# The first x and y tiles of an interleaving kernel, loaded in column halves in turn

## The chip, the cores and the metric

The kernel runs on one core of a Trainium2 chip. The metric is the device time of one execution in microseconds (us); lower is better. Times are medians of several runs; a profile is taken in one execution of its own.

## What is computed

Two float32 arrays x and y of shape (32, 256, 1024) are interleaved along the last axis, so that the result has 2048 columns:

```python
result = np.zeros((batch, seq, dim * 2), dtype=np.float32)
result[..., 0::2] = x
result[..., 1::2] = y
```

There is no arithmetic. Each input has 33.55 MB and the output 67.11 MB, so that 67.11 MB are read and 67.11 MB written.

## The kernel before

Each input is looked at as a flat run of numbers and cut into `n` = 8 tiles of 128 partitions by `W` = 8192 floats (32 KB in each partition, 4 MB in all). One tile of x and one of y give 8 MB of output, which is made in two halves: the half `h` (0 or 1) takes `H` = 4096 columns of x and of y and gives an output tile of 128 x 8192, 4 MB.

There are two buffers for x (`xt`), two for y (`yt`), used by even and odd tiles, and two for the output (`ot`), one for each half. Three engines run lists of their own, held together by semaphores:

- SP issues all loads. The x tile 0 comes in two column halves (L37 and L38, counted by `xsem[0]` and `hsem`), every other tile whole (x at L45, y at L48). From tile 2 on, a load of x waits until the third weave of the tile two before it is done, and a load of y until the fourth is, so that the buffer is free (L43 and L47).
- DVE weaves. For each tile and half, one copy spreads x to the even columns of `ot[h]` (L60) and one spreads y to the odd columns (L63). Ahead of the x copy it waits for the load of x and, from tile 1 on, for the store that last used `ot[h]` (L59); ahead of the first y copy of a tile it waits for the load of y (L62). Each copy counts `woven` up by one.
- ACT issues all stores (L68), one for each half, after the second copy of that half.

Each load and each store is spread over the core's 16 DMA engines, 8 of the 128 partition rows to each. In the profile q1 is the queue of SP's loads, and q10 that of ACT's stores.

After the program is built, the first two loads of SP are moved ahead of the barrier with which the program opens (L89 to L107); the loads after them are issued behind it.

Of the kernel before, what the change touches and what calls it, by code (L numbers as in the profile page):

```python
# [3 lines left out]


def _interleave(nc, x, y, out):
    P = 128
    W = 8192
    H = W // 2  # L10

    total = 1
    for s in x.shape:
        total *= s
    n = total // (P * W)
    assert n * P * W == total

    def rows(ap, names, k):
        flat = ap.rearrange("b s d -> (b s d)")
        return flat[k * names : (k + 1) * names].rearrange("(p w) -> p w", p=P)  # L20

    fp32 = mybir.dt.float32
    xt = [nc.alloc_sbuf_tensor(f"xt{b}", [P, W], fp32).ap() for b in (0, 1)]
    yt = [nc.alloc_sbuf_tensor(f"yt{b}", [P, W], fp32).ap() for b in (0, 1)]
    ot = [nc.alloc_sbuf_tensor(f"ot{b}", [P, W], fp32).ap() for b in (0, 1)]

    xsem = [nc.alloc_semaphore(f"xsem{b}") for b in (0, 1)]
    hsem = nc.alloc_semaphore("hsem")
    ysem = [nc.alloc_semaphore(f"ysem{b}") for b in (0, 1)]
    woven = nc.alloc_semaphore("woven")  # L30
    osem = [nc.alloc_semaphore(f"osem{b}") for b in (0, 1)]

    xs = [rows(x, P * W, k) for k in range(n)]
    ys = [rows(y, P * W, k) for k in range(n)]
    os_ = [rows(out, 2 * P * W, k) for k in range(n)]

    nc.sync.dma_start(out=xt[0][:, :H], in_=xs[0][:, :H]).then_inc(xsem[0], 16)  # L37
    nc.sync.dma_start(out=xt[0][:, H:], in_=xs[0][:, H:]).then_inc(hsem, 16)  # L38

    for k in range(n):  # L40
        b = k % 2
        if k >= 2:
            nc.sync.wait_ge(woven, 4 * (k - 2) + 3)  # L43
        if k:
            nc.sync.dma_start(out=xt[b], in_=xs[k]).then_inc(xsem[b], 16)  # L45
        if k >= 2:
            nc.sync.wait_ge(woven, 4 * (k - 2) + 4)  # L47
        nc.sync.dma_start(out=yt[b], in_=ys[k]).then_inc(ysem[b], 16)  # L48

    for k in range(n):  # L50
        b = k % 2
        for h in (0, 1):
            c = slice(h * H, (h + 1) * H)
            if h == 0:
                nc.vector.wait_ge(xsem[b], 16 * (k // 2 + 1))
            elif k == 0:
                nc.vector.wait_ge(hsem, 16)
            if k:
                nc.vector.wait_ge(osem[h], 16 * k)  # L59
            nc.vector.tensor_copy(out=ot[h][:, 0::2], in_=xt[b][:, c]).then_inc(woven, 1)  # L60
            if h == 0:
                nc.vector.wait_ge(ysem[b], 16 * (k // 2 + 1))  # L62
            nc.vector.tensor_copy(out=ot[h][:, 1::2], in_=yt[b][:, c]).then_inc(woven, 1)  # L63

    for k in range(n):
        for h in (0, 1):
            nc.scalar.wait_ge(woven, 4 * k + 2 * h + 2)
            nc.scalar.dma_start(  # L68
                out=os_[k][:, h * W : (h + 1) * W], in_=ot[h]
            ).then_inc(osem[h], 16)  # L70

    nc.scalar.wait_ge(osem[0], 16 * n)
    used = sorted(s.num for s in [*xsem, hsem, *ysem, woven, osem[0]])
    assert used == list(range(used[0], used[-1] + 1)), used
    nc.scalar.sem_clear(range(used[0], used[-1] + 1))
    nc.sync.nop(nofuse=True).wait_op(osem[1], 16 * n, "sem-ge").then_inc(
        osem[1], -16 * n
    )


def kernel(tc, x, y, out):
    nc = tc.nc
    tc.close()
    tc.compile()

    _interleave(nc, x, y, out)

    blocks = nc.main_func.blocks
    for engine in (mybir.EngineType.SP, mybir.EngineType.SP):  # L89
        opening = blocks[0].instructions  # L90
        at, moved = next(
            (b, i)
            for b in blocks[1:]
            for i in b.instructions
            if i.engine == engine and i.opcode == "DMACopy"
        )
        assert not (moved.sync_info and moved.sync_info.on_wait)
        body = at.instructions
        body.remove(moved)
        gate = next(  # L100
            n
            for n, i in enumerate(opening)
            if i.engine == engine and i.opcode == "Drain"
        )
        opening.insert(gate, moved)
        at.instructions = body
        blocks[0].instructions = opening  # L107


# [1 line left out]
_INS = ['x', 'y']  # L111
_OUTS = [((32, 256, 2048), 'float32')]


# [23 lines left out]
```

## Time and profile before

| | before |
|---|---|
| time, median of 3 runs | 314.31 us (314.28 to 314.42) |
| the profiled execution | 314.29 us |
| its span, first to last instruction | 313.0 us |
| DVE busy | 72.6 us (23%), 32 copies |
| one copy L60, L63 | 2295 ns, 2292 ns |
| DMA | 134.22 MB, mean 429 GB/s |
| loads (q1), stores (q10), share of the 16 DMA engines' span | 50.1%, 49.7% |
| DVE's idle time before L60, before L63 | 178.8 us, 46.7 us |

The span is what the profile covers; the time of an execution is a little longer. Nothing runs on TensorE. Idle time of DVE is put down to the transfer that ended it. In the windows view, each line gives a stretch of the span, its length, the busy time of the engines with their number of instructions, the clock, the mean busy share of the DMA engines and the rate in GB/s. The records of single packets, which lie under these views in the trace, give each packet's start, duration, size and queue.

The opening, by the timeline: the loads are issued at 0.00 and 0.42 (the x halves), 1.90 (y), 2.28 and 2.76 us (tile 1). DVE weaves the first x half from 7.30 and the first y half from 21.90, and the first store is issued at 24.23.

### The profile page before, as it was taken

The numbers are of one execution on the slowest core, as the hardware profiler recorded it, in microseconds if no ns is written. First come the engines' busy times: TensorE is split into PE (matmuls) and PEld (weight loads), VectorE is DVE, ScalarE is ACT, GpSimd is POOL, SyncE is SP. The second block draws the span as 40 slices with busy tenths as digits, with TensorE's granted clock in tenths as the row PEclk, the third lists the DMA queues.
The fourth block names the chain that finished last, engine by engine and source line by source line (L and its number), as shares of the span: only waits on it lengthen the run. The fifth ranks groups of instructions, "written<-read, shape, count | busy, mean of one in ns | idle before, by whom it ended". The sixth has DMA issues, their size and how long they took to land.

```text
span 313.0 us, 113 instructions
## 1 busy us (share of the span) xinstructions
DVE 72.6 (23%) x32; POOL 0.2 (0%) x4
## 2 busy tenths in 40 slices
DVE  0226002231022410325003150031501305013510
POOL 0000000000000000000000000000000000000000
DMA  8999999999999999999999999999999999999998
GB/s 341 463 410 394 469 402 448 423 436 436 419 452 406 465 402 469 402 469 402 469 402 448 423 436 436 419 452 406 465 402 469 402 469 402 465 406 444 427 431 373
DMA packets 4752, 134.22 MB, mean 429 GB/s; under 512 B 528, under 2 KB 528, under 8 KB 528
## 3 DMA queue, kind: packets, MB, share of 16 engines
q1 hardware_dynamic: 2448, 67.11, 50.1%
q10 hardware_dynamic: 2304, 67.11, 49.7%
HBM read 67.11 MB, written 67.11 MB: 429 GB/s over the span
## 4 chain that ended last, share of the span: by engine, by line
DMA 82%; DVE 12%; issue 0%
DMA out_dram<-ot 76%; DVE ot L63 6%; DMA yt<-in_y_dram 6%; DVE ot L60 6%
## 5 line engine op out<-in xcount | busy, mean ns | idle before, releaser
L60 DVE COPY ot<-xt 128x4096 f32<-128x4096 f32 x16 | 36.7, 2295 | 178.8 <-DMA out_dram<-ot 171.5
L63 DVE COPY ot<-yt 128x4096 f32<-128x4096 f32 x16 | 36.7, 2292 | 46.7 <-DMA yt<-in_y_dram 46.7
L122 POOL MEMSET const-bfloat16-1.0<- 128x1 bf16 x1 | 0.1, 101 | 0.0
L122 POOL MEMSET const-uint8-127<- 128x1 uint8 x1 | 0.1, 101 | 0.0
L122 POOL MEMSET const-float32-0.0<- 128x1 f32 x1 | 0.1, 98 | 0.2 <-issue 0.2
L122 POOL MEMSET const-float32-1.0<- 128x1 f32 x1 | 0.1, 98 | 0.0
## 6 DMA issues: line engine op xcount, KB each, us to landing
out_dram<-ot ACTq DMA_DIRECT2D x16, 4096.0 KB, 29.1
yt<-in_y_dram SPq DMA_DIRECT2D x8, 4096.0 KB, 60.8
xt<-in_x_dram SPq DMA_DIRECT2D x7, 4096.0 KB, 43.7
xt<-in_x_dram SPq DMA_DIRECT2D x2, 2048.0 KB, 9.5
```

What stands on the lines that cost most here:

```text
L60: nc.vector.tensor_copy(out=ot[h][:, 0::2], in_=xt[b][:, c]).then_inc(woven, 1)
L63: nc.vector.tensor_copy(out=ot[h][:, 1::2], in_=yt[b][:, c]).then_inc(woven, 1)
L122: nc = _bacc.Bacc("TRN2", target_bir_lowering=False, num_devices=1)
```

## The change

The first y tile is loaded in two column halves too, and the four halves come in the order x, y, x, y. The second y half has a semaphore of its own, `qsem`, and DVE waits for it ahead of the second y copy of tile 0. The whole load of y tile 0 in the loop falls away. The two loads that are moved ahead of the opening barrier are still the first two of SP, now the first x half and the first y half.

```diff
+    qsem = nc.alloc_semaphore("qsem")
...
     nc.sync.dma_start(out=xt[0][:, :H], in_=xs[0][:, :H]).then_inc(xsem[0], 16)
+    nc.sync.dma_start(out=yt[0][:, :H], in_=ys[0][:, :H]).then_inc(ysem[0], 16)
     nc.sync.dma_start(out=xt[0][:, H:], in_=xs[0][:, H:]).then_inc(hsem, 16)
+    nc.sync.dma_start(out=yt[0][:, H:], in_=ys[0][:, H:]).then_inc(qsem, 16)
...
-        nc.sync.dma_start(out=yt[b], in_=ys[k]).then_inc(ysem[b], 16)
+        if k:
+            nc.sync.dma_start(out=yt[b], in_=ys[k]).then_inc(ysem[b], 16)
...
             if h == 0:
                 nc.vector.wait_ge(ysem[b], 16 * (k // 2 + 1))
+            elif k == 0:
+                nc.vector.wait_ge(qsem, 16)
             nc.vector.tensor_copy(out=ot[h][:, 1::2], in_=yt[b][:, c]).then_inc(woven, 1)
...
-    used = sorted(s.num for s in [*xsem, hsem, *ysem, woven, osem[0]])
+    used = sorted(s.num for s in [*xsem, hsem, qsem, *ysem, woven, osem[0]])
```

## The prediction

> **What bounds the kernel now.** I read the page first: its rows of DMA and of DVE, the queues, then the groups of instructions.
>
> ```profile
> DVE 72.6 (23%) x32; POOL 0.2 (0%) x4
> DMA  8999999999999999999999999999999999999998
> DMA packets 4752, 134.22 MB, mean 429 GB/s; under 512 B 528, under 2 KB 528, under 8 KB 528
> q1 hardware_dynamic: 2448, 67.11, 50.1%
> q10 hardware_dynamic: 2304, 67.11, 49.7%
> L60 DVE COPY ot<-xt 128x4096 f32<-128x4096 f32 x16 | 36.7, 2295 | 178.8 <-DMA out_dram<-ot 171.5
> L63 DVE COPY ot<-yt 128x4096 f32<-128x4096 f32 x16 | 36.7, 2292 | 46.7 <-DMA yt<-in_y_dram 46.7
> ```
>
> DVE, the only engine that computes, is busy for 23% of the span and waits for transfers the rest of it. The DMA engines are busy in every slice, and the loads (q1) and stores (q10) fill 99.8% of them between them. So the question is not when a store may start but when the 16 engines are empty. The windows view, in stretches of 12.1 us, tells whether the mix of loads and stores matters (columns: stretch, length, DVE and POOL busy, clock, DMA share, GB/s):
>
> ```profile
> 12.00:24.10 12.10, 2.20 (x1) 0.00 (x0) 1.00 1.00 433
> 24.10:36.20 12.10, 4.50 (x3) 0.00 (x0) 1.00 0.96 390
> 48.30:60.40 12.10, 4.30 (x2) 0.00 (x0) 1.00 1.00 433
> 299.90:312.00 12.10, 0.00 (x0) 0.00 (x0) 1.00 1.00 433
> ```
>
> Loads alone (12 to 24), both together (48 to 60), stores alone (300 to 312): 433 GB/s each time. Only the stretch in which the first store joins the loads is slower. In steps of 1.21 us, the time of one 32 KB packet on an engine, it looks like this:
>
> ```profile
> 25.12:26.33 1.21, 1.21 (x2) 0.00 (x0) 1.00 1.11 433
> 26.33:27.54 1.21, 1.21 (x2) 0.00 (x0) 1.00 1.22 352
> 27.54:28.75 1.21, 1.06 (x1) 0.00 (x0) 1.00 0.27 81
> 28.75:29.96 1.21, 0.00 (x0) 0.00 (x0) 1.00 1.02 433
> ```
>
> There is one hole in the stream, just ahead of the first store packet (29.06 us; its store was issued at 24.23). The steps count packets by their start, so the view bounds the hole by one step, 1.21 us. The records of the single packets are finer: the last two load packets on each engine before the hole took on average 1.35 and 1.80 us instead of 1.213, and the first store packet 1.23. That is 0.14 + 0.58 + 0.02 = 0.74 us lost.
>
> **The account of the run before.** On each engine: first packet at 1.01 us; 256 steps of 1.2094 us (packet start to packet start) = 309.6; 33 small closing packets of 0.006 = 0.2; the first packets' slow start 0.58 (1.19 us on average for 16 KB that later take 0.611); the hole 0.74. Sum 312.1; the last packet ends at 312.58, the rest being the engines' spread (their first packets start over 0.5 us). Landing and closing make it 313.0, and 1.29 lies outside the span: 314.29, against a median of 314.31.
>
> **The change, part by part.** *Bytes and packets.* The same 134.22 MB. The first y tile comes in 16 KB packets, 16 per engine instead of 8 of 32 KB. The x halves of before show 16 KB packets 0.607 us apart: 16 x 0.607 - 8 x 1.2094 = +0.04, and one more closing packet 0.006. Together **+0.05 us**.
>
> *Issues.* L37 stays first at 0.00; the y half takes L38's place (0.42), the second x half that of the first y load (1.90), and the second y half comes one issue later, near 2.3, which pushes the loads of tile 1 back by 0.4 us. The two early halves keep the engines busy until 11.3 to 11.8 us, so everything issued by 3.7 us is covered by 7.6 us of queued work: 0. If that cover were gone, each issue would cost its 0.33 to 0.44 us.
>
> *The first store.* The y half lands where the second x half did (L38's landing, 12.16). Weave 2.3 us: store issued at 14.5 instead of 24.23, 9.7 us sooner. Its first packet comes 4.83 us after issue if it goes as before, or 3.6 if the two load packets ahead of it count 0.61 each instead of 1.21: at 18.1 to 19.3. No byte goes faster for that: from there the loads run at half pace, as in the mixed stretch. By the 433 GB/s of every mix this is 0. The new wait of DVE for the second y half holds nothing up but the second store.
>
> *What is late next: stores run out.* Before, both stores of tile 0 were issued by 28.65, and each later store while others were queued. After the change I walk it by packets, alternating between the queues as the records show in the mixed stretch. x, second half: packets end at 16.6, woven by 19.3. y, second half: 2 to 5 of its 8 packets are through when the store enters; each other one shares with a 32 KB store packet (0.61 + 1.21 = 1.82 us), ends 24.8 to 28.1, lands 1.59 later (y1: packets end 53.61, landed 55.20), woven 2.3 later: second store issued at 28.7 to 32.0. The first store's last packet starts 32.3 to 35.7. In the early corner the second store's issue comes only 0.3 us before that, and a store needed over 1 us from issue to engine: the store queue may run empty for 2 us here. Then, surely: the second store ends at 53 to 57, while the next needs the whole of y1. By then the engines have moved 32 steps of loads and 16 of stores: 1.6 + 48 x 1.21 + 0.74 = 60.4; landed 60.8, woven 63.1. So q10 is empty from about 55 until 66 to 68. The loads of tile 2 were long released (their weaves ended at 19.3 and about 31), so the engines go on at 433 GB/s, loads alone. But the store queue must be entered anew, once for sure and perhaps twice.
>
> *The price of an entry.* Only one is in the trace, 0.74 us. Another costs between 0 (the delay belonged to the very first use of the queue) and 1.21 us (the view's bound). I take 0.74: the hole lies where an empty queue's first packet has to come, and the other empty queue that is filled, that of loads at the start, shows a slow first packet of nearly the same size (0.58 lost), while transfers queued behind others show none. The first entry, now among 16 KB packets, I leave at 0.74; two shorter packets ahead could hide up to 1.21 less of it (worse), or it could vanish (better).
>
> *The end.* After its late entry the first store of tile 1 stands to the loads as the first store of tile 0 did before: woven from the last full y tile, 4.83 us after issue. So the rest repeats the old rhythm. Its last piece: store 15 of 16 was issued at 289.9, and store 14's last packet ended at 293.22, 3.3 us later, of which a fresh issue needs 1.0 (L37 to its first packet). The 2.3 us left cover it. Losing all of it and 2.3 more would cost 2.3; I count 0.
>
> **Sum:** 314.3 + 0.05 + 0.74 = **315.1 us** with one new entry, 315.8 with two.
>
> **Rivals.**
> *The entry costs only once per run* (the store queue's first use), so the refill is free: 314.3 + 0.05 = 314.35, no change. For it: one hole in the whole trace. Against: no other empty store queue is in the trace to compare. It decides from an entry price below 0.58 us (0.63 less 0.05).
> *Faster:* with smaller packets in flight the first entry finds a gap at once and loses nothing, and the later one is warm: 314.3 + 0.05 - 0.74 = 313.6. It needs both. Nothing shows the first.
> *The early store is worth its lead:* 9.7 us off, 304.6. The account excludes it: 309.6 us of packets do not fit.
> *Each added transfer pays a fixed cost* of an undrained queue, 1.01 from issue to packet and 0.36 from packet to landing: 315.7. The x halves speak against it: the second's packets follow the first's with one closing packet of 0.006 us between. The Trainium skill (DMA: Bandwidth & Descriptors, "Anatomy of one DMA — SWDGE (gpsimd) path") gives every transfer about 2.0 us fixed beside its bytes; taken for these loads too, as an estimate, the added split would make it 316.3. This trace shows that cost hidden for transfers that queue.
> *The change does not do what it says:* the early place goes to the first two loads of SP, now an x and a y half; DVE and ACT keep their order. Only a late y half would undo it.
>
> **How the numbers follow.** About 0.2% (0.63 us) can be told from no change here. New entries cost: 0.55, of which 0.05 at a price too small to tell. Free refill: 0.36. Faster: 0.04. Fixed cost, 0.03; a wider first hole alone, 0.02. The lead that pays and the undone change, under 0.01, are inside these. So faster 0.04, same 0.36 + 0.05 = 0.41, slower 0.50 + 0.03 + 0.02 = 0.55. The forecast is one new entry, 315.1. The range runs from the free refill less a little, 314.2, to two entries and some more at the first, 316.0; the slower case's own range is 314.9 to 316.0.
>
> **What would show it.** In the profile after: the first store issued near 14.5; 433 GB/s in all stretches but those around 17 and around 66 us (perhaps 35); a stretch near 60 with loads alone; the tail as before, with DVE's wait before its last weave near 3.8 us. No dip near 66 and 314.4 would be the first rival. Wrong altogether: a stretch under 433 GB/s in the steady part or after the last load, or a bandwidth above it anywhere.

## The result and the profile after

The changed kernel takes 314.86 us (median of 22 runs, 314.66 to 315.09), the kernel before 314.44 us beside it (22 runs). The ratio is 1.0014, 95% interval 1.0008 to 1.0020: slower by 0.42 us. The interval excludes 1, and yet this is less than the 0.2% (0.63 us) that the prediction set as the least that could be told from no change. The profiled execution took 314.66 us against 314.29.

The page of the changed kernel, the lines that answer to those of before (L65 and L70 are the weaves of x and y):

```profile
DMA  8999999999999999999999999999999999999998
DMA packets 4896, 134.22 MB, mean 428 GB/s; under 512 B 544, under 2 KB 544, under 8 KB 544
q1 hardware_dynamic: 2592, 67.11, 50.2%
q10 hardware_dynamic: 2304, 67.11, 49.6%
L65 DVE COPY ot<-xt 128x4096 f32<-128x4096 f32 x16 | 36.7, 2295 | 171.8 <-DMA out_dram<-ot 146.0
L70 DVE COPY ot<-yt 128x4096 f32<-128x4096 f32 x16 | 36.7, 2292 | 53.9 <-DMA yt<-in_y_dram 53.9
```

Little in it has moved but the packets: 144 more, 128 of them data and 16 closing ones. DVE waits as long as ever, 225.7 us against 225.5, with 7 us moved from the x weaves to the y weaves. The timeline of the opening shows that the change does what it says:

```profile
12.28 2.30 DVE L70 COPY ot<-yt 128x4096 f32<-128x4096 f32 x1 [2.56 <-DMA yt<-in_y_dram]
14.60 82.39 ACTq L75 DMA_DIRECT2D out_dram<-ot  x5
17.17 2.30 DVE L65 COPY ot<-xt 128x4096 f32<-128x4096 f32 x1 [2.60 <-DMA xt<-in_x_dram]
30.17 2.30 DVE L70 COPY ot<-yt 128x4096 f32<-128x4096 f32 x1 [10.70 <-DMA yt<-in_y_dram]
```

The first store is issued at 14.60 instead of 24.23. In the windows view, around the first store (steps of one packet time) and around the later refill of the store queue:

```profile
14.52:15.73 1.21, 0.05 (x1) 0.00 (x0) 1.00 1.01 433
15.73:16.94 1.21, 0.00 (x0) 0.00 (x0) 1.00 0.97 393
16.94:18.15 1.21, 0.98 (x1) 0.00 (x0) 1.00 1.28 311
18.15:19.36 1.21, 1.21 (x1) 0.00 (x0) 1.00 1.14 393
19.36:20.57 1.21, 0.11 (x1) 0.00 (x0) 1.00 0.66 284
...
65.21:66.42 1.21, 1.21 (x2) 0.00 (x0) 1.00 1.00 433
66.42:67.63 1.21, 1.21 (x1) 0.00 (x0) 1.00 1.00 433
67.63:68.84 1.21, 0.69 (x1) 0.00 (x0) 1.00 1.00 433
68.84:70.05 1.21, 0.00 (x0) 0.00 (x0) 1.00 1.00 433
```

The hole at the first store is there again: the four steps below 433 GB/s lack as much as the full stream moves in 0.98 us. At 68.14 us the first store packet of tile 1 enters a queue that had been empty since 53.99 us, and the stream does not falter.

For finer numbers I use the records of the single packets. *Loss* below is the time that has gone by, less the work of the packets done by then at their undisturbed spacing (1.2094 us for 32 KB, 0.607 for 16 KB, 0.006 for a closing packet, other sizes in proportion), as the mean of the 16 engines. What it grows by around a hole is what the hole costs. By it the last packet's end moves from 312.58 to 312.97 us, by 0.39:

| term | before | after | difference |
|---|---|---|---|
| the y split, 16 KB spacing and a closing packet | | | +0.05 |
| opening (loss at 8 us) | 1.84 | 1.91 | +0.07 |
| first store (growth) | 0.76 | 1.00 | +0.24 |
| refill at 68 us (growth) | none there | 0.00 | 0.00 |
| after the last load, to the last packet | 0.14 | 0.17 | +0.03 |

In four kernels below whose opening is that of the kernel before, the loss at 8 us is 1.87 to 1.96, each from one profile; the 0.07 is no larger than that scatter, and no run shows it to be an effect of the change. So the first store's hole is the large term, and the next question is what makes it 1.00 instead of 0.76.

### The profile page after: what moved, and what is told of

Same layout as the page of the kernel before. It is cut to its first block, busy times and chain, and to the rows that moved or that the text cites. A ratio compares the mean times of both kernels' runs of the same rounds, so it can differ in the third digit from the quotient of the medians.

```text
span 313.3 us, 114 instructions
## 1 busy us (share of the span) xinstructions
DVE 72.7 (23%) x32; POOL 0.2 (0%) x4
## 4 chain that ended last, share of the span: by engine, by line
DMA 79%; DVE 12%; another core or an unknown queue 4%; SPq 0%; issue 0%
DMA out_dram<-ot 65%; DMA xt<-in_x_dram 15%; DVE ot L65 6%; DVE ot L70 6%; SPq L42 0%; SPq L41 0%
## 5 line engine op out<-in xcount | busy, mean ns | idle before, releaser
L65 DVE COPY ot<-xt 128x4096 f32<-128x4096 f32 x16 | 36.7, 2295 | 171.8 <-DMA out_dram<-ot 146.0
L70 DVE COPY ot<-yt 128x4096 f32<-128x4096 f32 x16 | 36.7, 2292 | 53.9 <-DMA yt<-in_y_dram 53.9
```

## The experiments

Theories are numbered as they came up. The diffs show the lines that matter; `...` stands for lines left out, among them those that allocate a semaphore or count it. The kernel before, run beside them, had medians of 314.46 to 314.52 us.

### The store queue used earlier by a load

```diff
-    nc.sync.dma_start(out=xt[0][:, H:], in_=xs[0][:, H:]).then_inc(hsem, 16)
+    nc.scalar.dma_start(out=xt[0][:, H:], in_=xs[0][:, H:]).then_inc(hsem, 16)
```

> The kernel before, with the load of the second x half issued by ACT instead of SP, so that the store queue (q10) carries a load at about 2 us and is empty again well before the first store. Theory 1 (the hole is the price of the queue's very first use): no hole near 26 us; 0.75 us lost among the load packets near 3 us instead (time 314.4, as before) or nothing at all there (313.6). Theory 2 (the hole is the price of the first packet that goes from SBUF to DRAM, whatever its queue did before): hole of 0.75 us still at 26 us, time 314.4.

314.45 us, ratio 1.0003 (0.9994 to 1.0011). q10 carried the x half from 5.62 to 17.73 us (the second early place went to the load of y tile 0, at 0.41). The hole stands where it was, with a growth of 0.81:

```profile
26.40:27.61 1.21, 1.21 (x2) 0.00 (x0) 1.00 1.16 325
27.61:28.82 1.21, 1.03 (x1) 0.00 (x0) 1.00 0.36 108
```

Theory 1, the queue's first use, is out.

### A tiny store ahead of the first

```diff
+    warm = nc.alloc_sbuf_tensor("warm", [16, 128], fp32).ap()
+    nc.vector.memset(warm, 0.0).then_inc(wset, 1)
...
+    nc.scalar.wait_ge(wset, 1)
+    nc.scalar.dma_start(out=os_[0][:16, :128], in_=warm).then_inc(wsem, 16)
+    nc.scalar.wait_ge(wsem, 16)
...
```

> The kernel before, with a store of 16 rows of 512 bytes issued by ACT at about 2 us into a place that the first real store overwrites later. Theories 1 and 2 both say that the hole near 26 us is gone; what it cost is paid at the start. If the opening, in which the engines wait for their first data anyway, hides it: 313.7 to 313.9. If it is paid among the x packets at its full price: 314.4. Theory 3 (each filling of an empty store queue costs 0.74, as the prediction took it) says that the hole stays at 26 us and the tiny store adds one: 315.0.

314.44 us, ratio 1.0002 (0.9993 to 1.0011). Its 512-byte packets went out from 5.66 us without a visible loss, and the hole near 26 us stayed, 0.60. Theory 2, the first packet from SBUF to DRAM, is out. Theory 3 is hit too: the tiny store filled an empty queue and added no hole.

The same with 128 rows, so that each engine has used the partitions and output rows of the real store, from a buffer of its own and from `ot` itself (there DVE zeroes the 512 bytes first, and weaves only when the tiny store has landed):

> The kernel before, with a store of 128 rows of 512 bytes issued by ACT at about 2 us, from a tile of its own into the place that the first real store overwrites; so every engine has read its own partitions and written its own output rows before. Theory 4 (the hole is a first touch by each engine of its partitions or of its output rows): the hole near 26 us, 0.6 to 0.8 us in four kernels so far, is gone, 313.8. Theory 5 (a first touch of the output buffer ot as a source): the hole stays, 314.5. Theory 6 (the first store packet is late because of its own 32 KB, wherever it goes): the hole stays.

> As the run before it, but with the tiny store read from the first 512 bytes of each row of ot, the buffer of the first real store. Theories 4 and 5: the hole near 26 us is gone, 313.8 to 313.9. Theory 6: it stays, 314.5.

314.56 us (ratio 0.9996 to 1.0015) and 314.48 us (0.9994 to 1.0012); holes of 0.64 and 0.84. Theories 4 and 5, a first touch of rows or buffer, are out as far as 512 bytes of each row can touch them.

### The store queue emptied four times

```diff
             nc.scalar.wait_ge(woven, 4 * k + 2 * h + 2)
+            if h == 0 and 2 <= k <= 5:
+                nc.scalar.wait_ge(osem[1], 16 * k)
```

> The kernel before, with ACT waiting ahead of the first store of tiles 2, 3, 4 and 5 until the store before it has landed, so that the store queue runs empty four times beside queued loads. Theory 3 (each filling costs 0.74): +3.0 us, 317.4, with a hole in the stream at each. Theories 1 and 2 (only the first costs): within 0.2 us of before, 433 GB/s at each of the four refills, with loads alone for a few us ahead of each.

318.2 us, ratio 1.0122 (1.0108 to 1.0136). That is near Theory 3's time (317.4), and yet not for its reason. The first refill (110 us) and the third (196 us) grew the loss by 0.00, the second (153 us) by some 0.04. The packets show where it went: the load queue ran dry from 236.12 to 242.74 us, because its next loads were issued only at 237.56 and 239.76, behind weaves of which the first had waited 15.0 us for a store; the loss grew by 2.5 us from 230 to 260, and by 1.1 at the end, where the last packets of the 16 engines end between 315.2 and 316.6 us. Another 0.5 went between 128 and 220 us, apart from the refills; what took it is not known. The windows of the first refill, of this stretch and of the end:

```profile
104.00:116.10 12.10, 4.50 (x2) 0.00 (x0) 1.00 1.00 433
238.10:250.20 12.10, 1.63 (x1) 0.00 (x0) 1.00 1.00 387
304.00:316.10 12.10, 0.00 (x0) 0.00 (x0) 1.00 0.92 398
```

The median alone would have been read as a confirmation. The edit disturbed more than it was meant to; only its first three refills come beside loads that run on.

### The packets in flight

The load of x tile 1, which is in flight when the first store of the kernel before comes, in two halves:

```diff
-        if k:
+        if k == 1:
+            for c in range(2):
+                s = slice(c * 4096, (c + 1) * 4096)
+                nc.sync.dma_start(out=xt[b][:, s], in_=xs[k][:, s]).then_inc(psem, 16)
+        elif k:
...
```

> The kernel before, with the load of x tile 1 in two column halves, so that the load packets in flight when the first store comes have 16 KB, not 32. If the packets' size sets how much of the first store's delay is covered: the hole grows from 0.75 to 1.0 us, and with the split's 0.05 the time is +0.3, 314.7. If the size has no part in it and the hole of the changed kernel was longer because it came early: hole 0.75, time +0.05, 314.45.

The hole grew to 0.98, at 26 us, with the store issued at 24.31:

```profile
25.71:26.92 1.21, 1.21 (x2) 0.00 (x0) 1.00 1.23 420
26.92:28.13 1.21, 1.21 (x1) 0.00 (x0) 1.00 1.08 244
28.13:29.34 1.21, 0.55 (x1) 0.00 (x0) 1.00 0.93 379
29.34:30.55 1.21, 0.00 (x0) 0.00 (x0) 1.00 0.66 284
```

The early time is not needed for the wider hole; the smaller packets are enough. The time rose more than forecast, to 315.05 us, ratio 1.0019 (1.0010 to 1.0028), and the rest of it, 0.39, lies at the end:

```profile
291.21:292.42 1.21, 1.21 (x1) 0.00 (x0) 1.00 1.00 433
292.42:293.63 1.21, 0.45 (x1) 0.00 (x0) 1.00 0.19 81
293.63:294.84 1.21, 0.64 (x1) 0.00 (x0) 1.00 1.01 433
```

Beside 32 KB store packets, 16 KB load packets get a third of an engine instead of half (from 29 to 34 us, 43 load packets start and 41 store packets), so the loads end at 288.98 us instead of 285.96. Store 15 is issued at 292.90, store 14's last packet ends at 293.82, and 0.92 us is too little: the engines stand idle. This is the cushion at the end that the prediction put at 2.3 us, here used up.

The opposite, on the changed kernel: the whole load of x tile 1 ahead of the second halves, so that 32 KB packets are in flight when the early store comes:

```diff
     nc.sync.dma_start(out=yt[0][:, :H], in_=ys[0][:, :H]).then_inc(ysem[0], 16)
+    nc.sync.dma_start(out=xt[1], in_=xs[1]).then_inc(xsem[1], 16)
     nc.sync.dma_start(out=xt[0][:, H:], in_=xs[0][:, H:]).then_inc(hsem, 16)
...
-        if k:
+        if k >= 2:
             nc.sync.dma_start(out=xt[b], in_=xs[k]).then_inc(xsem[b], 16)
```

> The changed kernel, with the whole load of x tile 1 put between the first and the second halves, so that 32 KB load packets are in flight when the early first store comes. If the packets' size sets the first hole (as the run with x tile 1 in halves showed near 26 us): the hole falls from 1.00 to 0.75 us, and with it the time by 0.25, to 314.6. If the early time sets it: 1.00 stays, 314.86.

The hole fell to 0.76, as forecast, though the store came as early as in the changed kernel (first packet 19.45 us):

```profile
16.92:18.13 1.21, 0.00 (x0) 0.00 (x0) 1.00 1.47 433
18.13:19.34 1.21, 0.00 (x0) 0.00 (x0) 1.00 0.00 0
19.34:20.55 1.21, 0.00 (x0) 0.00 (x0) 1.00 1.00 433
...
43.00:55.10 12.10, 3.55 (x2) 0.00 (x0) 1.00 1.00 433
```

The last line is a refill: the store queue was empty from 34.41 to 48.54 us, and again nothing is lost. The times fall into two groups, 314.43 to 314.55 (six runs) and 315.10 to 315.94 (six); the profile, 314.47, is of the lower, and what makes the upper is not known. The median of 314.82 decides nothing.

The split without the turn-taking:

```diff
-    nc.sync.dma_start(out=yt[0][:, :H], in_=ys[0][:, :H]).then_inc(ysem[0], 16)
     nc.sync.dma_start(out=xt[0][:, H:], in_=xs[0][:, H:]).then_inc(hsem, 16)
+    nc.sync.dma_start(out=yt[0][:, :H], in_=ys[0][:, :H]).then_inc(ysem[0], 16)
```

> The changed kernel with its first four loads in the order x, x, y, y: the split alone, without the turn-taking; the first store then starts some 5 us later than in the changed kernel and 5 us sooner than before. If the cost comes from the 16 KB packets in flight and the split: first hole 1.0 us near 21 us, time as the changed kernel, 314.8 to 314.9. If it comes from the turn-taking or the early time: hole 0.75, 314.5.

It was a poor test. The store was issued at 19.55 us, and by its first packet (24.35) the loads in flight were those of x tile 1, 32 KB each; the hole was 0.75, as their size would have it, and by my wording this would have spoken for the turn-taking. The time missed both forecasts: 316.08 us, ratio 1.0045 (1.0031 to 1.0058), spread from 314.84 to 316.98. The profile, 315.08, has a refill at 67.16 us that did cost something, 0.48, and loses 0.31 us after the last load, where the kernel before loses 0.14. Why the split alone is slower than the changed kernel in most runs stays open.

### The store's own packets

The first store in two pieces, 8 KB and 24 KB of each row:

```diff
+            if k == 0 and h == 0:
+                for s in (slice(0, 2048), slice(2048, 8192)):
+                    nc.scalar.dma_start(
+                        out=os_[0][:, s], in_=ot[0][:, s]
+                    ).then_inc(fsem, 16)
+                continue
...
```

> The kernel before, with the first store in two pieces, 8 KB and then 24 KB of each row, so that the first store packet has 8 KB instead of 32. Theory 6 (the packet must be read before the engine can go on): the hole shrinks from 0.75 to about 0.2 us or less, 313.9. Theories 4 and 5: it stays at 0.6 to 0.8, 314.5.

The hole shrank to 0.40, and 0.17 more came at the step to the second piece: 314.22 us, ratio 0.9991 (0.9982 to 1.0000). Theory 6 holds in sign, not in size. With 2 KB and 30 KB (`slice(0, 512)`):

> The kernel before, with the first store in two pieces of 2 KB and 30 KB of each row. The piece of 8 KB left 0.40 us of hole and 0.16 us at the step to 24 KB. If the first packet's own size sets the hole: 0.3 us or less at the first piece, about 0.2 at the step to 30 KB; time 314.1 to 314.2. If the hole goes with the first packet of near 32 KB, wherever it stands: next to none at the first piece, 0.6 or more at the step; time 314.4.

0.02 at the first piece and 0.79 at the step to the second (its first packet at 39.47 us). The windows view of that stretch:

```profile
34.00:46.10 12.10, 0.00 (x0) 0.00 (x0) 1.00 0.96 387
```

314.38 us, ratio 0.9995 (0.9986 to 1.0003). The hole waits for the large packets, in a queue that by then is not empty. The same cut as the first, on the changed kernel (8 KB and 24 KB):

> The changed kernel, with its first store in two pieces of 8 KB and 24 KB of each row. If the store packet's own size is a part of the hole here too: 1.00 falls by about 0.35 to 0.65 us, and 0.1 to 0.2 comes at the second piece; time 314.6 to 314.7. If in this kernel the hole is set by the load packets alone: 1.00, 314.9.

1.00 fell to 0.47, and 0.24 more came at the step to the second piece (first packet at 27.72 us): 314.55 us, ratio 1.0003 (0.9994 to 1.0011), with 0.31 lost again at the end. So the size of the first store's packets counts in both kernels.

Is one large packet enough?

```diff
+        if k == 2:
+            nc.sync.wait_ge(wsem, 16)
...
+    nc.scalar.wait_ge(xsem[0], 16)
+    nc.scalar.dma_start(out=os_[0][:16, :H], in_=xt[0][:16, :H]).then_inc(wsem, 16)
+    nc.scalar.wait_ge(wsem, 16)
```

> The kernel before, with an early store of one 16 KB packet per engine (16 rows, raw x) as soon as the first x half is there, about 7.3 us; it writes a place that the first real store overwrites later. Theory 7 (only the first large store packet on an engine makes a hole): a hole near 10 us, and less than 0.2 us, or none, near 26; the time 0.6 us (one packet more) above before, 315.0. Theory 8 (the hole belongs to the first lasting stream of stores, not to a first packet): 0.6 to 0.8 us near 26 us as ever.

The one packet per engine at 10.9 us lost 0.03, and the hole near 26 us stayed, 0.61. That is as Theory 8 has it, the first lasting stream of stores. The time, 315.2 us (ratio 1.0011 to 1.0031), is 0.7 us above the kernel before, of which the added packet explains 0.6.

### The holes together

| load packets in flight | growth of loss at the first whole store, us |
|---|---|
| 32 KB, nine kernels | 0.60 to 0.84 |
| 16 KB: the changed kernel, x tile 1 in halves | 1.00, 0.98 |

The first row has before (0.76), the x half on ACT, the three tiny stores, the four gaps (0.65), x tile 1 first (0.76), the split alone (0.75) and the early large packet (0.61). The rows do not overlap, and the size was changed both ways, each time with the store's time left alone. Each figure is of one profile.

The same profiles show how the hole is made up. Beside 32 KB load packets the first store packet came 4.68 to 4.92 us after its issue, and less the hole that leaves 4.04 to 4.16 us in all nine: by this reckoning the loads ran on for that long. Beside 16 KB packets it came after 4.51 and 4.56 us, and the loads ran on for only 3.51 and 3.58: smaller packets cover half a microsecond less.

## Why the prediction was right or wrong

**What bounds the kernel: right.** 9.7 us of an earlier store bought nothing. Every stretch of loads alone, of both and of stores alone ran at 433 GB/s in the changed kernel too. Its 452 GB/s from 24.00 to 36.10 us is no rate above the bound: the view counts packets by their start, and the loss stays at 2.9 us over that stretch.

**The walk: mostly right.** First store issued at 14.60 (14.5 predicted), its first packet at 19.11 (18.1 to 19.3), the next tile's first store packet at 68.14 (66 to 68), and DVE's wait ahead of the last weaves as before, 3.76 us. The second y half came later than said: packets end at 28.58 (24.8 to 28.1), second store issued at 32.49. The queue did not visibly run empty for it: its first packet came 2.27 us after the first store's last packet ended, 2.10 in the undisturbed alternation.

**The price of an entry: wrong, and with it the forecast's main term.** The prediction put 0.74 us on the refill at 68 us and left the first entry as it was. The refill cost 0.00. The first entry cost 0.24 more, because 16 KB packets were in flight; the prediction had named this ("two shorter packets ahead could hide up to 1.21 less of it") and counted it as nothing, with 0.02 for it alone. So 0.05 + 0.24, and 0.07 of scatter in the opening, took the place of 0.05 + 0.74: the forecast of 315.1 us lay near the measured 314.86 by luck, with a wrong term inside. The first rival was right on the refill, though its reason, the queue's first use, was ruled out by the x half on ACT; its 314.35 missed the wider hole.

**Its reasoning on the price.** That "the hole lies where an empty queue's first packet has to come" was an argument from one event. Refills of the empty store queue beside loads cost 0.00 (the changed kernel at 68 us, x tile 1 first at 48, the gaps at 110 and 196), 0.04 (the gaps at 153) and 0.48 (the split alone at 67). An empty queue is not enough to make a hole. In the five refills beside loads that cost 0.04 at most, the first packet came 3.05 to 4.19 us after its issue, within the 4.04 to 4.16 that the loads covered at the first store, or nearly so; in the one that cost 0.48 it came after 4.47. Why the first store's packet takes longer is not shown.

**The other rivals.** A fixed cost of 1.4 us for each added transfer is out: the whole difference is 0.39 us, of which the packets of the split account for 0.05. The Trainium skill (DMA: Bandwidth & Descriptors, "Anatomy of one DMA — SWDGE (gpsimd) path") gives about 2.0 us fixed for each DMA on the GpSimd path. These loads are issued by SP and queue behind others, and no such cost shows in their time. The faster rival's smaller packets did the reverse of what it needed.

**Shown and open.** Shown: the hole of the first lasting stream of large stores grows when the load packets in flight get smaller and shrinks when its own first packets do. Not shown: why. Theory 6, that a store packet must first be read before the engine can go on, fits the sign of both, but no record here tells a packet's reading from its writing, and it does not tell why later entries of the same size were mostly free. This stays open, as do the two groups of times of x tile 1 first and the spread of the split alone.

## What to carry to other kernels

Where the DMA engines are full from the first packet to the last, as here, starting a transfer earlier buys nothing; ask only where the stream has holes, and what the edit does to each. A hole seen once in a trace has no price for a second one until a second one has been seen. And the end has a cushion that lies in the lead of the loads over the stores: an edit in the opening that shifts their shares, as the halves of x tile 1 did, can lose more 260 us later than where it was made.

## What the runs showed of the hardware

- Loads of 16 KB packets beside stores of 32 KB packets take turns packet by packet, so that the loads get a third of an engine (0.70 of 2.04 MB from 29 to 34 us in the kernel with x tile 1 in halves): its last load packets, of 32 KB again, ended 3.0 us later than in the kernel before, 0.2 of it by the wider hole.
- The version with the first store in pieces of 8 and 24 KB had the lowest median, 314.22 us, beside 314.46 for the kernel before; its interval, 0.9982 to 1.0000, reaches no difference.
- Refilling the load queue beside running stores was not free in the kernel with gaps: load packets start again at 242.74 us, and around it (241 to 244 us) 26 packets took longer than usual, 1.18 us in the mean over the engines.
